# FFN-down with ten of sixteen contraction pairs a sweep by seven products, in threes, with half of their weight sums made earlier and kept in HBM

## The chip, the cores and the metric

One core of one Trainium2 chip runs the whole program. The metric is the device time of one execution in microseconds (us), as the median of several runs.

## What is computed

One decoder layer over 256 tokens of width 2048 in float32. Its parts are a pooling and RWKV-7 mixer, a squared-ReLU MLP with inner width 8192, and a gated embedding behind it. Only the MLP changes, and of it mainly the second product:

```python
h2 = rms_norm(x, mlp_norm[i])
x = x + jnp.square(jax.nn.relu(h2 @ w_ffn_up[i])) @ w_ffn_down[i]
gate = jax.nn.sigmoid(rms_norm(x, ple_norm[i]) @ w_ple_gate[i])
x = x + gate * (p[i] @ w_ple_proj[i])
```

## The kernel before

**Three matmuls for one product.** Every float32 operand is split into a high part (ScalarE copies it to the type that TensorE takes, line 171 for weights) and a low part (VectorE subtracts the high part from the original, line 172). One product of two operands is then three matmuls: high by high, low by high, and high by low.

**The MLP in two halves.** `ffn_half` does FFN-up for half of the inner width (eight calls of `gemm_wide`, tiles `wh_u`, `wl_u`, lines 1121 and 1125), squares the result into 16 activation pairs that it keeps in SBUF, and then runs two sweeps of FFN-down, each for 1024 of the 2048 output columns. The sweeps are named d00, d01, d10 and d11 (half, then column block). In the trace all four share the name `d`.

**A sweep.** Its 16 pairs are 2 x 128 rows of the contraction each. For a pair two raw weight tiles of 128x1024 are loaded, `ra` with the blocks b11 and b22 and `rb` with b12 and b21. A *plain* pair takes eight products of 128x512, 24 matmuls. A pair in `SEVEN` is done in the manner of Strassen and Winograd: seven products, 21 matmuls, on sums of the activation blocks (made in `square_seven`) and on four sums of weight blocks (`weights_seven`). Before the change the odd pairs 1 to 13 are in `SEVEN`, so that a plain pair stands between any two. Within a seven TensorE first takes the three *block products* (p1, p2, p3, weights `w7h`, `w7l`) and then the four *sum products* (weights `th`, `tl`): eight matmuls with `th`, then four with `tl`. The sums are made in a tile `t` (lines 1244, 1247, 1248), its high parts `th` by ScalarE (1249, 1253), its low parts `tl` by VectorE (1254). There is one buffer each of `t`, `th` and `tl`.

**Rings.** Raw weight tiles come from a ring of five buffers, their high parts `wh` from a ring of five, their low parts `wl` from a ring of four. A tile gets the buffer of the one taken five (four) places earlier, so it waits until that one's last reader is done. SyncE's queue (SP) issues all the weight loads in order.

**PSUM.** A sweep adds up in four banks (p2, p3, p4, d22) and in two double banks w1 (p1, p6) and w2 (p5, p7). Behind the last seven the double banks are joined in a tile `u` (lines 1306 to 1308) and added to the residual stream `x` (line 1327, 128x1024). Behind the last pair the four banks are added to `x` (line 1327, 128x512), one by one. The next sweep takes the same four banks in the same order, so its first matmul on p2 waits until VectorE has taken p2 away.

**What sets the order.** From FFN-up on, a scheduler places the instructions on each engine in an order of its own, by priorities and by estimates of when each is ready. The engines then run that list strictly in order. An instruction that waits holds up all that is listed behind it on its engine.

## Time and profile before

| | us |
|---|---|
| median of three runs (lowest, highest) | 1178.73 (1176.62, 1181.19) |
| the profiled execution, its own time | 1176.96 |
| its span, first to last instruction | 1175.2 |
| TensorE busy in the span | 1159.9 |
| VectorE busy | 855.4 |
| ScalarE busy | 673.2 |

The profiled execution has 1.76 us outside its span and lies 1.77 us under the median of the runs. "PE" in the rows below is TensorE, "DVE" VectorE, "ACT" ScalarE, "SP" SyncE. Matmuls overlap: a 128x512 one is shown 389 ns long, but the distance from one to the next is shorter, so durations of matmuls are read from starts.

### The profile page before, as it was taken

What the parts mean: (1) busy time and instruction counts of PE and PEld (TensorE: products, weight loads), DVE (VectorE), ACT (ScalarE), POOL (GpSimd) and SP (SyncE); (2) the same over time, 40 slices, a digit from 0 to 9 for tenths busy, and PEclk for the clock granted to TensorE, in tenths of its full rate; (3) what the DMA queues carried; (4) which work ended last, traced back from release to release, by engine and by line L of the source; (5) the groups of instructions that cost most, each with busy time, mean ns of one, the idle gap of its engine ahead of it and who ended that gap; (6) DMA issues with size and microseconds to landing.
All of it is one profiled execution on the core that took longest, in us unless ns stands there. A gap on an engine that the chain in (4) does not pass through costs nothing.

```text
span 1175.2 us, 18983 instructions
## 1 busy us (share of the span) xinstructions
PE 1159.9 (99%) x7384; PEld 998.0 (85%) x7384; DVE 855.4 (73%) x1073; ACT 673.2 (57%) x1208; POOL 18.3 (2%) x77
## 2 busy tenths in 40 slices
...
GB/s 271 162 171 127 156 144 141 150 169 142 202 182 182 192 184 193 190 188 195 185 191 198 216 214 215 182 190 184 186 190 174 188 221 205 215 253 171 294 98 72
DMA packets 60906, 216.92 MB, mean 185 GB/s; under 512 B 6800, under 2 KB 7696, under 8 KB 60432
## 3 DMA queue, kind: packets, MB, share of 16 engines
...
## 4 chain that ended last, share of the span: by engine, by line
PE 86%; DVE 2%; ACT 1%; DMA 0%; issue 0%; DVEq 0%; ACTq 0%
PE u_w L1121 20%; PE d_p L1191 17%; PE u_w L1125 10%; PE d_w L1191 6%; PE d_d L1191 4%; PE o_b L194 2%; PE o_b L195 2%; PE o_b L193 2%; PE gt_b L193 2%; PE gt_b L195 2%; PE gt_b L194 2%; PE zp_b L193 1%; PE zp_b L195 1%; PE zp_b L194 1%; PE zv_b L184 1%; PE zv_b L186 1%
## 5 line engine op out<-in xcount | busy, mean ns | idle before, releaser
L1121 PE MATMUL u_w<-h,wh_u 128*128 128x512 f32 x1024 | 358.7, 395 | 0.0
L1125 PE MATMUL u_w<-h,wl_u 128*128 128x256 f32 x1024 | 287.3, 281 | 0.0
L171 ACT ACTIVATE wh_u<-raw_u 128x512 fp32r<-128x512 f32 x256 | 147.3, 624 | 157.7 <-issue 134.1
L172 DVE TENSOR_TENSOR wl_u<-raw_u,wh_u 128x1024 fp32r<-128x1024 f32 x128 | 156.4, 1224 | 101.9 <-PE u_w L1125 82.2
L1121 PEld LDWEIGHTS u_w<-h,wh_u 128*128 128x128 f32 x1024 | 192.0, 188 | 44.9
L1125 PEld LDWEIGHTS u_w<-h,wl_u 128*128 128x128 f32 x1024 | 193.5, 189 | 0.0
L171 ACT ACTIVATE wh_d<-raw_d 128x512 fp32r<-128x512 f32 x144 | 82.2, 622 | 64.4 <-PE d_d L1191 45.2
L1191 PE MATMUL d_p<-wh_d,yd 128*128 128x512 f32 x432 | 115.5, 389 | 0.0
L1191 PEld LDWEIGHTS d_p<-wh_d,yd 128*128 128x128 f32 x432 | 81.0, 188 | 16.8
L172 DVE TENSOR_TENSOR wl_d<-raw_d,wh_d 128x1024 fp32r<-128x1024 f32 x72 | 85.3, 1219 | 6.7 <-PE d_d L1191 4.7
L1254 DVE TENSOR_TENSOR tl_d<-t_d,th_d 128x2048 fp32r<-128x2048 f32 x28 | 64.1, 2290 | 16.6 <-ACT th_d L1253 16.6
L1191 PE MATMUL d_p<-wl_d,yd 128*128 128x512 f32 x216 | 66.5, 389 | 0.0
L172 DVE TENSOR_TENSOR wl_o<-raw_o,wh_o 128x1024 fp32r<-128x1024 f32 x32 | 39.1, 1223 | 37.5 <-PE o_b L195 21.8
L171 ACT ACTIVATE wh_o<-raw_o 128x512 fp32r<-128x512 f32 x64 | 36.9, 624 | 38.6 <-issue 17.8
L1191 PEld LDWEIGHTS d_p<-wl_d,yd 128*128 128x128 f32 x216 | 40.5, 188 | 8.5
L1243 ACT ACTIVATE w7h_d<-raw_d 128x1024 fp32r<-128x1024 f32 x28 | 29.5, 1054 | 26.8 <-PE d_d L1191 25.4
L1244 DVE TENSOR_TENSOR t_d<-raw_d,raw_d 128x1024 f32<-128x1024 f32 x28 | 34.2, 1221 | 14.6 <-DMA raw_d<-in_w_ffn_down_dram 14.5
L1191 PE MATMUL d_w<-th_d,ys 128*128 128x512 f32 x168 | 42.6, 389 | 0.0
L1249 ACT ACTIVATE th_d<-t_d 128x1024 fp32r<-128x1024 f32 x28 | 29.7, 1062 | 20.5 <-ACT wh_d L171 8.4
L1253 ACT ACTIVATE th_d<-t_d 128x1024 fp32r<-128x1024 f32 x28 | 29.5, 1053 | 20.6 <-DVE t_d L1248 20.6
L172 DVE TENSOR_TENSOR wl_zp<-raw_zp,wh_zp 128x1024 fp32r<-128x1024 f32 x16 | 19.5, 1221 | 26.0 <-ACT wh_zp L171 24.8
L1191 PE MATMUL d_d<-wh_d,yd 128*128 128x512 f32 x144 | 38.5, 389 | 0.0
...
## 6 DMA issues: line engine op xcount, KB each, us to landing
raw_u<-in_w_ffn_up_dram SPq DMA_DIRECT2D x128, 512.0 KB, 3.5
raw_d<-in_w_ffn_down_dram SPq DMA_DIRECT2D x128, 512.0 KB, 4.3
raw_o<-in_w_out_dram SPq DMA_DIRECT2D x32, 512.0 KB, 3.6
raw_gt<-in_w_ple_gate_dram SPq DMA_DIRECT2D x24, 512.0 KB, 4.6
raw_zk<-in_w_in_dram SPq DMA_DIRECT2D x16, 512.0 KB, 3.5
raw_zr<-in_w_in_dram SPq DMA_DIRECT2D x16, 512.0 KB, 3.5
raw_zv<-in_w_in_dram SPq DMA_DIRECT2D x16, 512.0 KB, 3.5
raw_zp<-in_w_in_dram SPq DMA_DIRECT2D x16, 512.0 KB, 3.5
```

What stands on the lines that cost most here:

```text
L171: nc.scalar.activation(wh[:, a * 512 : (a + 1) * 512], raw[:, a * 512 : (a + 1) * 512], AF.Copy)
L172: nc.vector.tensor_tensor(wl, raw, wh.bitcast(F32), op=ALU.subtract)
L193: nc.tensor.matmul(o, a_h, wh[:, 0:n], start=first, stop=False)
L194: nc.tensor.matmul(o, a_l, wh[:, 0:n], start=False, stop=False)
L195: nc.tensor.matmul(o, a_h, wl[:, 0:n], start=False, stop=last)
L1121: nc.tensor.matmul(bank[:, ct, :].rearrange("p (s t) -> p s t", s=2), wh[:, c], hl, start=k == 0, stop=False, skip_group_check=True,)
L1125: nc.tensor.matmul(bank[:, ct, 0:T], wl[:, c], hl[:, 0, :], start=False, stop=k == 15, skip_group_check=True)
L1191: nc.tensor.matmul(o, l, r, start=first, stop=last, skip_group_check=True)
L1243: nc.scalar.activation(ha, ra, AF.Copy)
L1244: nc.vector.tensor_tensor(t[:, 0:2], ra.rearrange("p (c n) -> p c n", c=2), b12.unsqueeze(1).to_broadcast([128, 2, 512]), op=ALU.subtract)
L1249: nc.scalar.activation(th[:, 0:2], t[:, 0:2], AF.Copy)
L1254: nc.vector.tensor_tensor(tl, t, th.bitcast(F32), op=ALU.subtract)
```

## The change

`SEVEN` becomes all pairs but 0, 3, 6, 9, 12 and 15: ten a sweep, and two of them now follow each other without a plain pair between. Of each two neighbours the second (2, 5, 8, 11, 14, named `AHEAD`) no longer makes its weight sums in the sweep. `sums_ahead` makes them during FFN-up: it loads both raw tiles through the raw ring, makes the four sums on VectorE in a tile that shares the buffer of `th`, and writes them, 1 MB, to a DRAM tile. The sweep reads them back as two raw tiles, and reads only half of `rb`. The first neighbour (1, 4, 7, 10, 13) makes its sums in place, over the raw tiles, after their low parts are taken. The first neighbour does its sum products first and its block products after, the second the other way round. `t` is gone. `u` (and the scratch tile of `rms_stat`) share the buffer of `tl` instead. The activation sums are made in place as well. The weights that `keep` holds for the last gate product are put into other buffers, and their low parts are made in two instructions instead of one.

```diff
-    SEVEN = tuple(range(1, 14, 2))
-    F_A11, F_A12, F_A22, F_S1, F_S3, F_S2, F_S4 = range(7)
+    PLAIN = tuple(range(0, 16, 3))
+    AHEAD = tuple(range(2, 16, 3))
+    SEVEN = tuple(i for i in range(16) if i not in PLAIN)
+    dr = ctx.enter_context(tc.tile_pool(name="dr", bufs=1, space=bass.MemoryType.DRAM))
+    saved = {}
...
+    def sums_ahead(hf, np_, i):
+
+        ra, rb = (
+            load_raw(w_down[np_, hf * 16 + i, r].rearrange("p a n -> p (a n)"), 1024, f"ta{hf}{np_}_{i}_{r}") for r in range(2)
+        )
+        b11, b22, b12, b21 = ra[:, 0:512], ra[:, 512:1024], rb[:, 0:512], rb[:, 512:1024]
+        t = fp.tile([128, 4, 512], F32, tag="th", name=f"ta{hf}{np_}_{i}")
+        with tc.high_priority(20000):
+            nc.vector.tensor_tensor(
+                t[:, 1:3], ra.rearrange("p (c n) -> p c n", c=2)[:, ::-1], b12.unsqueeze(1).to_broadcast([128, 2, 512]),
+                op=ALU.subtract,
+            )
+            nc.vector.tensor_tensor(t[:, 0], b11, t[:, 1], op=ALU.add)
+            nc.vector.tensor_tensor(t[:, 3], b21, t[:, 0], op=ALU.subtract)
+        d_ = saved[hf, np_, i] = dr.tile([128, 2, 1024], F32, tag=f"ta{hf}{np_}_{i}", name=f"tad{hf}{np_}_{i}")
+        nc.sync.dma_start(d_.rearrange("p r n -> p (r n)"), t.rearrange("p c n -> p (c n)"))
+    F_A11, F_A12, F_A22, F_S2, F_S3, F_S4, F_S1 = range(7)
 
...
     def square_seven(src, pr):
 
-        y = fp.tile([128, 1792], F32R, tag="ys", bufs=7, name=f"ys{pr}")
+        if pr == SEVEN[-1]:
+            y = a8(5, f"ys{pr}", F32R)[:, 0:1792]
+        else:
+            y = fp.tile([128, 1792], F32R, tag="ys", bufs=9, name=f"ys{pr}")
         yh, yl = (y[:, c : c + 896].rearrange("p (f t) -> p f t", t=128) for c in (0, 896))
         k1t0, k1t1, k2t0, k2t1 = (src[:, c * 128 : (c + 1) * 128] for c in range(4))
-        sf = fp.tile([128, 4, 128], F32, tag="u", name=f"sf{pr}")
-        nc.vector.tensor_tensor(sf[:, 0], k1t1, k2t1, op=ALU.add)
-        nc.vector.tensor_tensor(sf[:, 1], k1t0, k1t1, op=ALU.subtract)
-        nc.vector.tensor_tensor(sf[:, 2], sf[:, 0], k1t0, op=ALU.subtract)
-        nc.vector.tensor_tensor(sf[:, 3], k2t0, sf[:, 2], op=ALU.subtract)
         tok0 = src.rearrange("p (k t) -> p k t", k=2)[:, :, 0:128]
         split_sb(yh[:, 0:2], yl[:, 0:2], tok0)
         split_sb(yh[:, 2], yl[:, 2], k2t1)
-        split_sb(yh[:, 3:7], yl[:, 3:7], sf)
+        nc.vector.tensor_tensor(k2t1, k1t1, k2t1, op=ALU.add)
+        nc.vector.tensor_tensor(k1t1, k1t0, k1t1, op=ALU.subtract)
+        nc.vector.tensor_tensor(k1t0, k2t1, k1t0, op=ALU.subtract)
+        nc.vector.tensor_tensor(k2t0, k2t0, k1t0, op=ALU.subtract)
+        split_sb(yh[:, 3:7], yl[:, 3:7], src.rearrange("p (f t) -> p f t", t=128))
...
-    def weights_seven(ra, rb, name):
-
-        b12, b21, b22 = rb[:, 0:512], rb[:, 512:1024], ra[:, 512:1024]
-        t, th, tl = (
-            fp.tile([128, 4, 512], dt, tag=tg, name=f"{tg}_{name}") for tg, dt in (("t", F32), ("th", F32R), ("tl", F32R))
-        )
+    def weights_seven(ra, rb, tr, name):
+
+        b11, b22, b12, b21 = ra[:, 0:512], ra[:, 512:1024], rb[:, 0:512], rb[:, 512:1024]
+        th, tl = (fp.tile([128, 2, 1024], F32R, tag=tg, name=f"{tg}_{name}") for tg in ("th", "tl"))
         ha, hb = (ring("wh", F32R, f"w7h{i}_{name}") for i in range(2))
         la, lb = (ring("wl", F32R, f"w7l{i}_{name}") for i in range(2))
         with tc.high_priority(20000):
             nc.scalar.activation(ha, ra, AF.Copy)
-            nc.vector.tensor_tensor(
-                t[:, 0:2], ra.rearrange("p (c n) -> p c n", c=2), b12.unsqueeze(1).to_broadcast([128, 2, 512]), op=ALU.subtract
-            )
-            nc.vector.tensor_tensor(t[:, 2], b22, t[:, 0], op=ALU.add)
-            nc.vector.tensor_tensor(t[:, 3], b21, t[:, 2], op=ALU.subtract)
-            nc.scalar.activation(th[:, 0:2], t[:, 0:2], AF.Copy)
             nc.scalar.activation(hb[:, 0:512], b21, AF.Copy)
             nc.vector.tensor_tensor(la, ra, ha.bitcast(F32), op=ALU.subtract)
             nc.vector.tensor_tensor(lb[:, 0:512], b21, hb[:, 0:512].bitcast(F32), op=ALU.subtract)
-            nc.scalar.activation(th[:, 2:4], t[:, 2:4], AF.Copy)
-            nc.vector.tensor_tensor(tl, t, th.bitcast(F32), op=ALU.subtract)
+            if tr is None:
+                nc.vector.tensor_tensor(b22, b22, b12, op=ALU.subtract)
+                nc.vector.tensor_tensor(b12, b11, b12, op=ALU.subtract)
+                nc.vector.tensor_tensor(b11, b11, b22, op=ALU.add)
+                nc.vector.tensor_tensor(b21, b21, b11, op=ALU.subtract)
+                tr = (ra, rb)
+            for r in range(2):
+                nc.scalar.activation(th[:, r], tr[r], AF.Copy)
+            for r in range(2):
+                nc.vector.tensor_tensor(tl[:, r], tr[r], th[:, r].bitcast(F32), op=ALU.subtract)
 
...
+            kept_sums = saved.get((hf, np_, i))
+            ra = load_raw(src[np_, i, 0].rearrange("p a n -> p (a n)"), 1024, f"{name}_0_{i}")
+            if kept_sums is None:
+                rb, tr = load_raw(src[np_, i, 1].rearrange("p a n -> p (a n)"), 1024, f"{name}_1_{i}"), None
+            else:
+                rb = ring("raw", F32, f"raw_{name}_1_{i}")
+                nc.sync.dma_start(rb[:, 512:1024], src[np_, i, 1, :, 1])
+                tr = [load_raw(kept_sums[:, r], 1024, f"{name}_{2 + r}_{i}") for r in range(2)]
             if i in SEVEN:
-                w = weights_seven(ra, rb, f"{name}_{i}")
+                w = weights_seven(ra, rb, tr, f"{name}_{i}")
                 a = acts[i]
                 fin = i == last_seven
-                for which, o, f, t in (("p1", p1, F_A11, "b11"), ("p2", p2, F_A12, "b21"), ("p3", p3, F_S4, "b22")):
-                    put(which, o, a(f), w[t], fin and which == "p1")
-                for step in (put_high, put_low):
-                    for which, o, f, t in (
-                        ("p5", p5, F_S1, "t1"), ("p7", p7, F_S3, "t3"), ("p6", p6, F_S2, "t2"), ("p4", p4, F_A22, "t4")
-                    ):
-                        step(which, o, a(f), w[t], fin and which != "p4")
+                blocks = [("p1", p1, F_A11, "b11"), ("p2", p2, F_A12, "b21"), ("p3", p3, F_S4, "b22")]
+                sums_ = [("p5", p5, F_S1, "t1"), ("p7", p7, F_S3, "t3"), ("p6", p6, F_S2, "t2"), ("p4", p4, F_A22, "t4")]
+
+                def of_blocks():
+                    for which, o, f, t in blocks:
+                        put(which, o, a(f), w[t], fin and which == "p1")
+
+                def of_sums():
+                    for step in (put_high, put_low):
+                        for which, o, f, t in sums_:
+                            step(which, o, a(f), w[t], fin and which != "p4")
+
+                for part in (of_sums, of_blocks) if i + 1 in SEVEN else (of_blocks, of_sums):
+                    part()
                 if fin:
-                    u = fp.tile([128, 4, 512], F32, tag="t", name=f"u_{name}")
+                    u = fp.tile([128, 4, 512], F32, tag="tl", name=f"u_{name}")
...
             if f == 1:
                 inv_ms()
+            for j in range(i * 5 // 4, (i + 1) * 5 // 4):
+                sums_ahead(hf, j // 5, AHEAD[j % 5])
 
```

VectorE where sweep d00 ends and d01 begins, before. `u_d00` joins the double banks, `x0` and `x1` are the residual stream of the two token blocks, `d00_p2` to `d00_d22` the four banks, `wl_d01_0_0` and `wl_d01_1_0` the low parts for the first pair of d01, and `w7l0_d01_1` that of `ra` for its pair 1. `[waits ...]` names the engines or DMA queues that the row waits for.

```order
L1306 TENSOR_TENSOR u_d00_6540<-d00_w1_5978,u_d00_6540 128x512 [waits Activation_49]
L1307 TENSOR_TENSOR u_d00_6540<-d00_w2_5979,u_d00_6540 128x512 [waits DVE_49]
L1308 TENSOR_TENSOR u_d00_6540<-u_d00_6540,d00_w2_5979 128x2x512 [waits DVE_49]
L1327 SCALAR_TENSOR_TENSOR x0_3441<-u_d00_6540,s2sq_4301,x0_3441 128x1024 [waits DVE_49]
L1327 SCALAR_TENSOR_TENSOR x1_3442<-u_d00_6540,s2sq_4301,x1_3442 128x1024
L172 TENSOR_TENSOR wl_d01_0_0_6638<-raw_d01_0_0_6633,wh_d01_0_0_6637 128x1024 [waits DMAHW1_49,PE_49]
L172 TENSOR_TENSOR wl_d01_1_0_6643<-raw_d01_1_0_6635,wh_d01_1_0_6642 128x1024 [waits DMAHW2_49,PE_49,Activation_49]
L1327 SCALAR_TENSOR_TENSOR x0_3441<-d00_p2_5974,s2sq_4301,x0_3441 128x512 [waits DVE_49,PE_49]
L1327 SCALAR_TENSOR_TENSOR x0_3441<-d00_p3_5975,s2sq_4301,x0_3441 128x512 [waits PE_49]
L1244 TENSOR_TENSOR t_d01_1_6675<-raw_d01_0_1_6671,raw_d01_1_1_6673 128x1024 [waits DMAHW4_49,DMAHW3_49,DVE_49]
L1327 SCALAR_TENSOR_TENSOR x1_3442<-d00_p4_5976,s2sq_4301,x1_3442 128x512 [waits PE_49]
L1327 SCALAR_TENSOR_TENSOR x1_3442<-d00_d22_5977,s2sq_4301,x1_3442 128x512 [waits PE_49]
```

The same place after the change:

```order
L1345 TENSOR_TENSOR u_d00_6720<-d00_w1_6098,u_d00_6720 128x512 [waits Activation_49]
L172 TENSOR_TENSOR wl_d01_0_0_6780<-raw_d01_0_0_6775,wh_d01_0_0_6779 128x1024 [waits DMAHW1_49,Activation_49]
L1346 TENSOR_TENSOR u_d00_6720<-d00_w2_6099,u_d00_6720 128x512 [waits DVE_49]
L172 TENSOR_TENSOR wl_d01_1_0_6785<-raw_d01_1_0_6777,wh_d01_1_0_6784 128x1024 [waits DMAHW2_49,Activation_49]
L1347 TENSOR_TENSOR u_d00_6720<-u_d00_6720,d00_w2_6099 128x2x512 [waits DVE_49]
L1268 TENSOR_TENSOR w7l0_d01_1_6821<-raw_d01_0_1_6813,w7h0_d01_1_6819 128x1024 [waits DMAHW3_49,PE_49,Activation_49]
L1366 SCALAR_TENSOR_TENSOR x0_3441<-u_d00_6720,s2sq_4301,x0_3441 128x1024 [waits DVE_49]
L1366 SCALAR_TENSOR_TENSOR x1_3442<-u_d00_6720,s2sq_4301,x1_3442 128x1024
L1366 SCALAR_TENSOR_TENSOR x0_3441<-d00_p2_6094,s2sq_4301,x0_3441 128x512 [waits DVE_49]
L1366 SCALAR_TENSOR_TENSOR x0_3441<-d00_p3_6095,s2sq_4301,x0_3441 128x512
L1366 SCALAR_TENSOR_TENSOR x1_3442<-d00_p4_6096,s2sq_4301,x1_3442 128x512 [waits DVE_49]
L1366 SCALAR_TENSOR_TENSOR x1_3442<-d00_d22_6097,s2sq_4301,x1_3442 128x512
```

The two low parts for d01's first pair moved in among the three joins, `w7l0_d01_1`, which stood behind all rows on `x`, moved ahead of all six, and it waits for TensorE: its buffer in the ring of four is that of `wl_d00_0_15`, which the last matmul of d00 reads.

VectorE in the middle of sweep d00, before, around pairs 6 and 7 (`t_d00_7` are the sums of pair 7):

```order
L1244 TENSOR_TENSOR t_d00_7_6262<-raw_d00_0_7_6258,raw_d00_1_7_6260 128x1024 [waits DMAHW7_49,DMAHW0_49,DVE_49]
L1247 TENSOR_TENSOR t_d00_7_6262<-raw_d00_0_7_6258,t_d00_7_6262 128x512 [waits DVE_49]
L172 TENSOR_TENSOR wl_d00_0_6_6225<-raw_d00_0_6_6220,wh_d00_0_6_6224 128x1024 [waits DMAHW5_49,PE_49]
L1248 TENSOR_TENSOR t_d00_7_6262<-raw_d00_1_7_6260,t_d00_7_6262 128x512 [waits DVE_49]
L172 TENSOR_TENSOR wl_d00_1_6_6230<-raw_d00_1_6_6222,wh_d00_1_6_6229 128x1024 [waits DMAHW6_49,PE_49,Activation_49]
L1251 TENSOR_TENSOR w7l0_d00_7_6267<-raw_d00_0_7_6258,w7h0_d00_7_6265 128x1024 [waits PE_49]
L1252 TENSOR_TENSOR w7l1_d00_7_6268<-raw_d00_1_7_6260,w7h1_d00_7_6266 128x512 [waits Activation_49]
L1254 TENSOR_TENSOR tl_d00_7_6264<-t_d00_7_6262,th_d00_7_6263 128x2048 [waits PE_49,Activation_49]
L1244 TENSOR_TENSOR t_d00_9_6342<-raw_d00_0_9_6338,raw_d00_1_9_6340 128x1024 [waits DMAHW4_49,DMAHW3_49,DVE_49]
```

After, at pairs 7 and 8 (`raw_d00_0_7` and `raw_d00_1_7` as outputs are the sums in place, `tl_d00_8` are low parts of sums read back):

```order
L1271 TENSOR_TENSOR raw_d00_0_7_6386<-raw_d00_0_7_6386,raw_d00_1_7_6388 128x512 [waits DVE_49]
L1272 TENSOR_TENSOR raw_d00_1_7_6388<-raw_d00_0_7_6386,raw_d00_1_7_6388 128x512 [waits DVE_49]
L1268 TENSOR_TENSOR w7l0_d00_8_6441<-raw_d00_0_8_6429,w7h0_d00_8_6439 128x1024 [waits DMAHW3_49,PE_49,Activation_49]
L1273 TENSOR_TENSOR raw_d00_0_7_6386<-raw_d00_0_7_6386 128x512 [waits DVE_49]
L1269 TENSOR_TENSOR w7l1_d00_8_6442<-raw_d00_1_8_6431,w7h1_d00_8_6440 128x512 [waits DMAHW4_49,PE_49,Activation_49]
L1274 TENSOR_TENSOR raw_d00_1_7_6388<-raw_d00_1_7_6388,raw_d00_0_7_6386 128x512 [waits DVE_49]
L1279 TENSOR_TENSOR tl_d00_7_6391<-raw_d00_0_7_6386,th_d00_7_6390 128x1024 [waits Activation_49]
L1279 TENSOR_TENSOR tl_d00_7_6391<-raw_d00_1_7_6388,th_d00_7_6390 128x1024 [waits Activation_49]
L172 TENSOR_TENSOR wl_d00_1_9_6482<-raw_d00_1_9_6474,wh_d00_1_9_6481 128x1024 [waits DMAHW6_49,PE_49,Activation_49]
L1279 TENSOR_TENSOR tl_d00_8_6438<-raw_d00_2_8_6433,th_d00_8_6437 128x1024 [waits DMAHW5_49,PE_49,Activation_49]
L1268 TENSOR_TENSOR w7l0_d00_10_6518<-raw_d00_0_10_6510,w7h0_d00_10_6516 128x1024 [waits DMAHW7_49,Activation_49]
L1279 TENSOR_TENSOR tl_d00_8_6438<-raw_d00_3_8_6435,th_d00_8_6437 128x1024 [waits DMAHW0_49,Activation_49]
```

The low parts of pair 8 (`w7l0_d00_8`, `w7l1_d00_8`) now stand between the second and the fourth sum of pair 7, and the first of them waits for the buffer of `wl_d00_0_6`, which the plain pair 6 reads to its end. In sweeps d01 and d11 all four sums and `tl` of the first neighbour stand ahead of the second neighbour's rows.

SyncE's queue in FFN-up after the change, around the first saved sums (`raw_ta00_2_0` and `_1` are the loads, `tad00_2` the write). Before, only the `raw_u` rows stand there.

```order
L163 DMA raw_ta00_2_0_4512<-in_w_ffn_down_dram 128x1024 [waits DMAHW4_49,DVE_49]
L163 DMA raw_ta00_2_1_4514<-in_w_ffn_down_dram 128x1024 [waits DMAHW5_49,DVE_49,Activation_49]
L163 DMA raw_u10_0_4523<-in_w_ffn_up_dram 128x1024 [waits DMAHW6_49,DVE_49,Activation_49]
L163 DMA raw_u10_1_4546<-in_w_ffn_up_dram 128x1024 [waits DMAHW1_49,DVE_49]
L163 DMA raw_u10_2_4569<-in_w_ffn_up_dram 128x1024 [waits DMAHW7_49,DVE_49]
L1213 DMA tad00_2_4520<-ta00_2_4516 128x2048 [waits DVE_49]
L163 DMA raw_u10_3_4592<-in_w_ffn_up_dram 128x1024 [waits DMAHW0_49,DVE_49]
L163 DMA raw_u11_0_4631<-in_w_ffn_up_dram 128x1024 [waits DMAHW2_49]
```

The write is listed behind the loads that still find a free buffer of the ring; the load behind it takes the buffer that these sums give back.

44 lines of the change are left out of this document (22 added, 22 removed).

## The prediction

> **What bounds the kernel now.** I read the table of stretches first, then the chain of waits, the groups, the DMA issues, and the order in time at the end of a sweep.
>
> ```profile
> 554.05:636.40 82.35, 82.35 (x365) 68.16 (x364) 69.62 (x67) 45.09 (x66) 0.00 (x0) 1.00 0.58 197
> 636.40:718.60 82.20, 82.20 (x364) 68.05 (x364) 73.37 (x70) 46.09 (x67) 0.00 (x0) 1.00 0.62 208
> 718.60:899.54 180.94, 180.94 (x1026) 157.00 (x1025) 122.39 (x157) 94.00 (x174) 0.00 (x0) 1.00 0.61 188
> 1085.00:1125.00 40.00, 40.00 (x178) 33.15 (x177) 29.98 (x31) 27.84 (x52) 0.00 (x0) 1.00 0.85 286
> 1166.00:1168.00 2.00, 0.89 (x8) 0.68 (x6) 0.47 (x2) 1.00 (x2) 0.00 (x0) 1.00 0.01 2
> 1168.00:1170.00 2.00, 0.00 (x0) 0.00 (x0) 1.66 (x6) 1.76 (x5) 0.00 (x0) 0.73 0.00 0
> ```
>
> Each row has the stretch, its length, busy us of PE, PE's weight loads, DVE, ACT and POOL, the granted clock, the DMA engines' share and GB/s. The first two rows are the sweeps d00 and d01, the third FFN-up of the second half, the fourth a piece of the gate product. TensorE is busy for the whole of every sweep and of FFN-up, so it is the bound there, and a matmul less is time less as long as it stays so. VectorE is next: 70 to 73 of 82 us in a sweep.
>
> ```profile
> 630.93 4.08 PE d_p L1191 x18
> 635.01 1.36 PE d_d L1191 x6
> ...
> L1191 PE MATMUL d_p<-wh_d,yd 128*128 128x512 f32 x432 | 115.5, 389 | 0.0
> ```
>
> In the chain 18 matmuls of a plain pair take 4.08 us: 0.2267 each from start to start, though one is shown 0.389 long. A plain pair is 24 of them, 5.44 us; a seven is 21, 4.76 us (sums 12, 2.72; blocks 9, 2.04).
>
> **What the change saves.** Ten sevens instead of seven, three matmuls less in each of three pairs, four sweeps: 36 x 0.2267 = 8.2 us off, if TensorE never waits.
>
> **VectorE in a sweep.** Durations from the groups:
>
> ```profile
> L172 DVE TENSOR_TENSOR wl_d<-raw_d,wh_d 128x1024 fp32r<-128x1024 f32 x72 | 85.3, 1219 | 6.7 <-PE d_d L1191 4.7 <-ACT wh_d L171 1.9
> L1254 DVE TENSOR_TENSOR tl_d<-t_d,th_d 128x2048 fp32r<-128x2048 f32 x28 | 64.1, 2290 | 16.6 <-ACT th_d L1253 16.6
> L1244 DVE TENSOR_TENSOR t_d<-raw_d,raw_d 128x1024 f32<-128x1024 f32 x28 | 34.2, 1221 | 14.6 <-DMA raw_d<-in_w_ffn_down_dram 14.5
> L1247 DVE TENSOR_TENSOR t_d<-raw_d,t_d 128x512 f32<-128x512 f32 x28 | 19.2, 687 | 0.4
> L1251 DVE TENSOR_TENSOR w7l_d<-raw_d,w7h_d 128x1024 fp32r<-128x1024 f32 x28 | 34.1, 1218 | 0.4 <-PE u_w L1125 0.4
> L1252 DVE TENSOR_TENSOR w7l_d<-raw_d,w7h_d 128x512 fp32r<-128x512 f32 x28 | 19.1, 683 | 0.0
> L171 ACT ACTIVATE wh_d<-raw_d 128x512 fp32r<-128x512 f32 x144 | 82.2, 622 | 64.4 <-PE d_d L1191 45.2 <-issue 9.4 <-DMA raw_d<-in_w_ffn_down_dram 7.9
> L1249 ACT ACTIVATE th_d<-t_d 128x1024 fp32r<-128x1024 f32 x28 | 29.7, 1062 | 20.5 <-ACT wh_d L171 8.4 <-PE d_p L1191 3.6 <-DVE t_d L1244 3.6
> ```
>
> A seven before: 1.22 + 2 x 0.69 + 1.22 + 0.68 + 2.29 = 6.8 us; plain 2 x 1.22 = 2.44. A sweep 7 x 6.8 + 9 x 2.44 = 69.5 us of 82.3. After, a first neighbour has four sums of 128x512 (2.75), the low parts (1.90) and two of 128x1024 (2.44), 7.1 us; a second one only 1.90 + 2.44 = 4.3. A sweep is 5 x 7.1 + 5 x 4.3 + 6 x 2.44 = 71.8 us of 80.2: fuller (90% against 85%), and not the bound by its sum.
>
> **A triple in the steady order (d01, d11).** Take the first neighbour's sums on TensorE at 0, its blocks to 4.76, the second's blocks to 6.8 and sums to 9.52, the plain pair to 14.96. Back to back a 128x1024 costs VectorE 1.13 (2.35 for two, below). The raw buffers close a loop: the first neighbour's last low part frees the buffer of the next plain pair's first load. From there to the next such low part it takes 4.3 (landing, below), 1.2 (two high parts of 0.62), 3.4 (three low parts of 1.13), 0.6 (one of 128x512), 1.9 (three sums), 1.06 (the first `th`) and 2.35 (two low parts): 14.8, against 14.96. So these sweeps stand at balance, with little slack. I take 0.5 us lost in each, 1 us for both (bounds 0, and 0.3 a triple, 3 us for ten).
>
> ```profile
> raw_u<-in_w_ffn_up_dram SPq DMA_DIRECT2D x128, 512.0 KB, 3.5
> raw_d<-in_w_ffn_down_dram SPq DMA_DIRECT2D x128, 512.0 KB, 4.3
> raw_gt<-in_w_ple_gate_dram SPq DMA_DIRECT2D x24, 512.0 KB, 4.6
> ```
>
> **The end of d00 and of d10, the largest term.** VectorE and TensorE there before:
>
> ```profile
> 627.10 0.68 DVE L1306 TENSOR_TENSOR u_d<-d_w,u_d 128x512 f32<-128x512 f32 x1
> 627.82 0.69 DVE L1307 TENSOR_TENSOR u_d<-d_w,u_d 128x512 f32<-128x512 f32 x1
> 628.55 1.22 DVE L1308 TENSOR_TENSOR u_d<-u_d,d_w 128x1024 f32<-128x1024 f32 x1
> 629.80 2.48 DVE L1327 SCALAR_TENSOR_TENSOR x<-u_d,s2sq,x 128x1024 f32<-128x1024 f32 x2
> 632.20 2.35 DVE L172 TENSOR_TENSOR wl_d<-raw_d,wh_d 128x1024 fp32r<-128x1024 f32 x2
> 634.47 1.40 DVE L1327 SCALAR_TENSOR_TENSOR x<-d_p,s2sq,x 128x512 f32<-128x512 f32 x2
> 637.59 0.74 DVE L1327 SCALAR_TENSOR_TENSOR x<-d_d,s2sq,x 128x512 f32<-128x512 f32 x1
> ...
> 636.21 1.07 PE L1191 MATMUL d_p<-wh_d,yd 128*128 128x512 f32 x4
> 641.65 0.61 PE L1191 MATMUL d_w<-w7h_d,ys 128*128 128x512 f32 x2
> ```
>
> d01 begins on TensorE at 636.21. Its first bank, p2, was taken away by 634.47 + 0.74 = 635.2, one microsecond ahead; two plain pairs, 10.9 us, lay behind the last seven, and the joins had that long. Now the last seven is pair 14 and one plain pair, 5.44 us, is left; and in the new list `w7l0_d01_1` stands ahead of all six rows on `x` and waits for the last matmul of d00. Call the end of d00 E. Then: 0.2 (that matmul's end, 0.389 less 0.227 behind its successor's place), 1.13 for `w7l0`, 2.4 for the two wide `x`, 0.74 for p2: p2 is free at E + 4.5, and TensorE, whose next row is d01's first matmul on p2, waits 4.5 us. The other three banks follow 0.66 apart and TensorE needs them 1.36 apart. Behind that it goes on: p3, p4, d22 to E + 6.5, the low part of `rb` to 7.1, four sums to 9.7, the two `th` of 1.06 to 11.0, while the plain pair is over at 4.5 + 5.44 = 9.95. Pair 1 now wants its sums first, where before its blocks gave 2.04 us: one more wait of 1.1 us. Together 5.6 us, at two places: 11.2. Bounds: below, without the wait for TensorE, the joins from E - 5.4 with the two `wl` among them end at E - 0.5, and 2.4 + 0.74 more give 2.7 us a place; above, one low part more ahead of them, 6.8 us. I take the strict reading of the list, 5.6, since VectorE in the rows above runs its rows one behind the other too.
>
> **The other ends.** Behind d11 the first product of the embedding takes p2. VectorE has the joins from about E - 4.7 (`u` now shares the buffer of `tl`, which pair 14's last matmul reads), two `wl` among them, then the wide `x` and p2: 0.7 + 0.7 + 1.2 + 2 x 1.13 + 2.4 + 0.74 = 8.0, so E + 3.3, less 0.7 of transposes that TensorE now does meanwhile: 2.6 us (bounds 0, all of it hidden, and 3.3). Behind d01 FFN-up needs only the double banks: E + 6.5 + 1.1 for `wl_u80_3`, wanted at E + 3 x 2.83 = 8.5 (180.94 us for 64 raw tiles): nothing, with 0.9 us of cover.
>
> **The first sweeps, d00 and d10.** The list lets low parts of the second neighbour stand between the first's sums. At pair 7: `w7l0_d00_8` waits for the plain pair's end (0 here), then 1.13, a sum 0.6, 0.6, a sum 0.7, and the second `th` 1.05: ready at 4.4, while TensorE has done four of the six block products by 2.72 and wants the first `th` then: 1 to 1.5 us lost. At pair 8 TensorE's new list takes what is ready first and I find no wait. I take 1.5 us a sweep, 3 in all (bounds 0 and 1.5 a triple, 15).
>
> **FFN-up.**
>
> ```profile
> L1226 DVE TENSOR_TENSOR sf<-sf,r 128x128 f32<-128x128 f32 x7 | 2.0, 283 | 0.0
> ```
>
> A saved sum costs VectorE 1.22 + 2 x 0.69 = 2.6 us, ten a half, 26; three more activation pairs with four sums of 0.28 and a split of 0.7, 5.5: 122.4 becomes 154 of 180.9, hidden behind TensorE. The ring must bring 84 raw tiles instead of 64, one each 2.15 us, and SyncE's queue has ten writes of 1 MB between; each waits for its sums, and the load behind it needs the buffer of these sums anyway. The piece of the gate product above runs one raw tile each 2.0 us at full TensorE. Bytes: (84 x 0.524 + 10 x 1.05) MB / 180.9 us = 301 GB/s against 188. The same row shows 286 GB/s, all reads, at a share of 0.85. If 286 were all there is, a half would take 190.6 us, 9.7 more, 19 for both. I take 0.5 us, since an earlier stretch (10 to 20 us) shows more:
>
> ```profile
> 10.00:20.00 10.00, 9.51 (x44) 7.59 (x43) 8.26 (x16) 5.80 (x14) 8.59 (x20) 1.00 0.87 347
> ```
>
> In a sweep the load is (16 x 1.05 + 5 x 0.79) MB / 80.2 us = 258 GB/s, below both. The five activation sums in place, `junk` and the other buffers of `keep` cost nothing that I can see: ScalarE and VectorE have idle time in both places (94 and 122 of 181 us busy).
>
> **Sum.** -8.2 + 11.2 + 2.6 + 3 + 1 + 0.5 = +10.1 us. Against the profiled execution's 1176.96 this is 1187.1; the runs' median is 1.8 higher, and I set 1188.
>
> **Rivals.**
> - *TensorE stays fed, faster.* For: no engine's sum exceeds its stretch, and no row of the sweeps before has TensorE waiting. Against: p2's cover before was 1 us and 5.44 us of cover are taken off. It decides itself at p2's release: if that comes before E, the whole 8.2 us are kept: 1169 to 1171.
> - *No change.* Both ends cost their lower bound, 2 x 2.7, the third 1, the rest 1: 7.4 against 8.2, so 1176 to 1179.
> - *Transfers.* FFN-up is starved at 286 GB/s: up to 19 us more, 1195 to 1207. For: the ring is short by two buffers during saved sums. Against: the 347 GB/s row.
> - *The clock.* In the row from 1166 TensorE is busy for 0.89 us and then stops, and in the row from 1168 the granted clock is 0.73. If it falls in each of the three longer waits and stays so for as long as the wait, 4.5 x 0.27 = 1.2 us more at each, partly hidden by the wait for `th`: 1 to 4 us, 1189 to 1192.
>
> By the Trainium skill ("TensorE: Matmul & The Clock Gate", Part 1: The HAM clock gate) the clock is halved after about 3.4 us of idleness and needs as long a busy stretch to come back. By that rule, as an estimate from this page, a wait of 4.5 us may cost up to 1.7 us more, and three of them 5, which would make 1193. The granted-clock rows agree that it falls within 3 us of idleness; no row shows how it comes back.
>
> **Chances.** A measurement of this kernel tells a change from none at about 0.5%, 5.9 us: under 1172.8 is faster, over 1184.6 slower. Forecast 0.42, clock 0.14, transfers 0.08: slower 0.64. No change 0.22. Faster 0.14. The range of eight in ten leaves out most of the faster case and the upper part of the transfers: 1174 to 1199. It takes in the bounds of the ends (2.7 to 6.8 us each) and first sweeps of up to 5 us each.
>
> **What would show it.** TensorE waiting for VectorE's `x<-d_p` twice, 4 to 5 us each, some 80 us behind each FFN-up, and then about 1 us for `th`; a wait of 2 to 3 us behind d11; matmuls in the sweeps at 0.2267 us and 36 fewer; FFN-up still 181 us. I am wrong if `x<-d_p` ends ahead of the sweep's end, if TensorE idles inside the triples by more than 5 us a sweep, or if FFN-up is longer.

## The result, and the profile after

| | us | against the kernel before |
|---|---|---|
| kernel before, median (lowest, highest) | 1178.66 (1176.62, 1181.19) | |
| changed kernel, median (lowest, highest) | 1231.82 (1229.69, 1234.82) | 1.0452, 95% interval 1.042 to 1.0484 |
| span of the profiled execution, before and after | 1175.2 and 1228.7 | +53.5 |

The change makes the kernel 53 us slower. The direction was forecast, the size was not: 10 us were. The head of the page of the changed kernel, with its DMA issues:

```profile
span 1228.7 us, 19262 instructions
...
PE 1177.2 (96%) x7348; PEld 991.6 (81%) x7348; DVE 927.2 (75%) x1225; ACT 699.4 (57%) x1220; POOL 18.3 (1%) x77
...
raw_u<-in_w_ffn_up_dram SPq DMA_DIRECT2D x128, 512.0 KB, 5.6
raw_d<-in_w_ffn_down_dram SPq DMA_DIRECT2D x108, 512.0 KB, 5.4
...
raw_d<-tad SPq DMA_DIRECT2D x40, 512.0 KB, 4.5
```

The 36 matmuls are gone (7348 of 7384). A raw tile of weights in a sweep now takes 5.4 us to land by the median, where the page of before has 4.3; a tile of saved sums (`tad`) takes 4.5.

The table of stretches of the changed kernel, cut where one stage ends and the next begins. The columns are those of the prediction's first fence: stretch, length, busy us of PE, PE's weight loads, DVE, ACT and POOL, granted clock, DMA share, GB/s.

```profile
375.07:556.81 181.74, 181.74 (x1032) 157.70 (x1033) 147.21 (x206) 97.71 (x185) 0.00 (x0) 1.00 0.80 285
556.81:652.52 95.71, 84.43 (x357) 64.98 (x355) 77.94 (x84) 54.17 (x70) 0.00 (x0) 0.99 0.70 244
652.52:740.91 88.39, 85.32 (x355) 67.20 (x355) 72.33 (x77) 50.36 (x66) 0.00 (x0) 0.97 0.66 229
740.91:922.66 181.75, 181.16 (x1026) 156.86 (x1024) 148.14 (x204) 92.53 (x175) 0.00 (x0) 1.00 0.83 288
922.66:1022.48 99.82, 85.38 (x356) 64.74 (x355) 79.95 (x86) 54.83 (x71) 0.00 (x0) 1.00 0.71 236
1022.48:1111.53 89.05, 85.09 (x354) 66.63 (x355) 72.12 (x78) 50.18 (x65) 0.00 (x0) 0.98 0.64 226
1111.53:1228.70 117.17, 105.41 (x513) 88.69 (x511) 72.73 (x106) 68.44 (x134) 0.00 (x0) 0.95 0.49 168
```

The lengths of the same stages, side by side (from such tables of each kernel; "six buffers" is the first experiment below; a sweep runs to the next stage's first matmul, so a wait at its end counts with it):

| stage | before | after | six buffers |
|---|---|---|---|
| FFN-up, first half | 178.42 | 181.74 | 178.38 |
| d00 | 82.32 | 95.71 | 84.34 |
| d01 | 82.28 | 88.39 | 86.58 |
| FFN-up, second half | 180.89 | 181.75 | 181.17 |
| d10 | 82.34 | 99.82 | 83.54 |
| d11 | 82.28 | 89.05 | 83.99 |
| the rest, to the end | 111.20 | 117.17 | 113.63 |

All four sweeps are longer, though each has nine matmuls less: 354 x 0.2267 = 80.25 us is what TensorE needs for one. TensorE is busy in FFN-up but for 0.6 us, with the loads in at 285 to 288 GB/s, so it isn't starved. TensorE's waits, from the list of waits (engine, line, what it waited for, us in all, times, longest):

```profile
PE d_w L1217 <- ACT th_d L1277: 17.7, 23, 2.5
PE d_p L1217 <- DVE x L1366: 9.0, 2, 4.5
PE pp_b L193 <- DVE x L1366: 3.0, 1, 3.0
PE d_p L1217 <- ACT wh_d L171: 1.9, 3, 1.1
PE d_p L1217 <- DVE wl_d L172: 1.9, 4, 1.0
...
```

The second and third row are the ends of the sweeps, as forecast: 4.5 us twice, and 3.0 behind d11. The first row is new in size. The rows count only time in which no matmul is shown, so the sweeps lose more than these rows add up to: the last matmul ahead of a wait is shown 0.39 us long, and behind one for `th` the second starts 0.34 us after the first. What `th` itself waits for is seen in the chain of waits. One triple of d01 in it, in order of time (start, us, what):

```profile
679.12 5.76 DMA raw_d<-in_w_ffn_down_dram
...
684.96 1.08 ACT w7h_d L1266
...
686.06 0.14 DVE w7l_d L1268
686.20 1.00 issue
687.20 0.68 DVE w7l_d L1269
687.89 0.61 DVE raw_d L1271
...
688.52 0.70 DVE raw_d L1272
...
689.25 0.70 DVE raw_d L1273
...
690.06 1.07 ACT th_d L1277
...
691.15 0.92 DVE tl_d L1279
...
692.11 1.43 PE d_w L1217 x5
693.54 0.45 PE d_p L1217 x2
694.00 0.65 PE d_w L1217 x3
694.65 0.61 DVE w7l_d L1269
...
695.28 6.42 DMA raw_d<-in_w_ffn_down_dram
```

It is a loop. A load lands after 5.8 us, high part, low parts, three sums, `th`, the sum products and the second neighbour's low part follow, and that low part frees the buffer for the same load of the next triple: 695.28 - 679.12 = 16.2 us, where TensorE needs 14.96. One triple of d00:

```profile
580.02 1.22 DVE w7l_d L1268
581.24 1.15 DVE tl_d L1279
...
582.40 5.23 DMA raw_d<-tad
...
587.66 1.07 ACT th_d L1277
...
588.77 1.20 PE d_w L1217 x4
589.97 0.46 PE d_p L1217 x2
590.42 0.46 PE d_w L1217 x2
590.88 4.32 PE d_p L1217 x19
595.20 1.15 PE d_d L1217 x5
...
596.43 1.24 DVE w7l_d L1268
```

Here a saved sum is read (5.2 us) into the buffer that the first neighbour's first `tl` frees; that `tl` stands behind the second neighbour's low part, which waits for the plain pair's last matmul. Again one load in every turn, 596.43 - 580.02 = 16.4 us.

### The profile page after: what moved, and what is told of

Same layout as the page of the kernel before. It is cut to its first block, busy times and chain, and to the rows that moved or that the text cites. A ratio compares the mean times of both kernels' runs of the same rounds, so it can differ in the third digit from the quotient of the medians.

```text
span 1228.7 us, 19262 instructions
## 1 busy us (share of the span) xinstructions
PE 1177.2 (96%) x7348; PEld 991.6 (81%) x7348; DVE 927.2 (75%) x1225; ACT 699.4 (57%) x1220; POOL 18.3 (1%) x77
## 4 chain that ended last, share of the span: by engine, by line
PE 61%; DMA 12%; DVE 10%; ACT 4%; issue 2%; ACTq 0%; DVEq 0%; SPq 0%
PE u_w L1121 17%; DMA raw_d<-in_w_ffn_down_dram 9%; PE u_w L1125 9%; PE d_p L1217 5%; PE d_w L1217 3%; DMA raw_d<-tad 2%; PE o_b L194 2%; PE o_b L193 2%; PE o_b L195 2%; PE gt_b L194 2%; PE gt_b L195 2%; PE gt_b L193 2%; ACT th_d L1277 2%; PE zp_b L193 1%; PE zp_b L195 1%
## 5 line engine op out<-in xcount | busy, mean ns | idle before, releaser
L1277 ACT ACTIVATE th_d<-raw_d 128x1024 fp32r<-128x1024 f32 x80 | 82.7, 1055 | 95.8 <-DVE raw_d L1273 35.9
L1279 DVE TENSOR_TENSOR tl_d<-raw_d,th_d 128x1024 fp32r<-128x1024 f32 x80 | 96.3, 1223 | 40.3 <-ACT th_d L1277 40.1
L1217 PE MATMUL d_p<-wh_d,yd 128*128 128x512 f32 x288 | 82.2, 405 | 11.0 <-DVE x L1366 9.0
L1217 PE MATMUL d_w<-th_d,ys 128*128 128x512 f32 x240 | 68.8, 407 | 17.7 <-ACT th_d L1277 17.7
L172 DVE TENSOR_TENSOR wl_d<-raw_d,wh_d 128x1024 fp32r<-128x1024 f32 x48 | 58.5, 1224 | 25.4 <-ACT wh_d L171 23.6
L1217 PEld LDWEIGHTS d_p<-wh_d,yd 128*128 128x128 f32 x288 | 55.2, 195 | 25.2 <-issue 9.8
L1217 PEld LDWEIGHTS d_w<-th_d,ys 128*128 128x128 f32 x240 | 42.0, 188 | 38.4 <-ACT th_d L1277 31.7
L171 ACT ACTIVATE wh_d<-raw_d 128x512 fp32r<-128x512 f32 x96 | 55.0, 624 | 30.6 <-DMA raw_d<-in_w_ffn_down_dram 30.2
L1217 PE MATMUL d_p<-w7h_d,ys 128*128 128x512 f32 x160 | 50.1, 390 | 1.1 <-ACT w7h_d L1267 1.1
L1268 DVE TENSOR_TENSOR w7l_d<-raw_d,w7h_d 128x1024 fp32r<-128x1024 f32 x40 | 48.9, 1222 | 1.9 <-PE d_d L1217 1.1
```

Of the source, the lines that this page charges most:

```text
L171: nc.scalar.activation(wh[:, a * 512 : (a + 1) * 512], raw[:, a * 512 : (a + 1) * 512], AF.Copy)
L172: nc.vector.tensor_tensor(wl, raw, wh.bitcast(F32), op=ALU.subtract)
L1217: nc.tensor.matmul(o, l, r, start=first, stop=last, skip_group_check=True)
L1268: nc.vector.tensor_tensor(la, ra, ha.bitcast(F32), op=ALU.subtract)
L1277: nc.scalar.activation(th[:, r], tr[r], AF.Copy)
L1279: nc.vector.tensor_tensor(tl[:, r], tr[r], th[:, r].bitcast(F32), op=ALU.subtract)
```

## The experiments

The theories. **A, the ring**: eight raw tiles a triple go through five buffers, and the loss in the sweeps is the wait for a buffer and then for the load. **B**: the single buffers `th` and `tl`, shared by neighbours. **C**: VectorE's order. **D**: what was written to HBM comes back slowly. **Q**: SyncE's one queue holds loads up. Ratios are against the kernel before, on the same chip.

**1. A sixth raw buffer**

```diff
-    RING = {"raw": (3, 2), "wh": (3, 2), "wl": (3, 1)}
+    RING = {"raw": (3, 3), "wh": (3, 1), "wl": (3, 1)}
```

> The changed kernel with a sixth raw buffer; the room for it comes from the ring of high parts, which goes from five to four. Ring theory (A): in every triple one load is on the path, because the buffer it needs comes free only when the first neighbour's last low part is made, and it then takes 5 to 6.4 us to land where I had put 4.3. A sixth buffer lets that load be issued one buffer earlier; of the some 35 us that the four sweeps lose inside the triples 20 to 30 come back: 1200 to 1212 us. Theory B (the single buffers th and tl, shared by two neighbours, hold up the second one) and theory C (VectorE's rows stand in an order that makes it wait): a raw buffer changes neither, 1226 to 1236 us. In the new list the first low part of the new sweep also stands behind the six x rows at the two sweep ends; by the term of my prediction that alone is 1.1 us at each.

Measured: 1190.31 us, 1.0107 (1.0078 to 1.0136): 41 us back. Inside the sweeps, by the table of stages and without the waits for `x` and the half clock behind them, it is 27 us, as A expected; the rest is shorter waits for `x` (2.31 and 1.22 us instead of 4.52 twice), less time at half clock, and a faster FFN-up (4 us, last section). The shares of the chain, first of the changed kernel, then of this one, and this one's chain in d00:

```profile
PE 61%; DMA 12%; DVE 10%; ACT 4%; issue 2%; ACTq 0%; DVEq 0%; SPq 0%
```

```profile
PE 70%; DVE 9%; DMA 4%; ACT 3%; issue 2%; DVEq 0%; ACTq 0%
```

```profile
586.63 4.31 PE d_p L1217 x19
...
601.59 4.31 PE d_p L1217 x19
...
616.55 4.31 PE d_p L1217 x19
```

DMA falls from 12% to 4% of the chain, and in d00 the plain pair now comes each 14.96 us, which is TensorE's own time for a triple to the last digit. In d01 loads stay in the chain, and d01 and d11 still lose 4.6 and 3.7 us. The transfer rate is not what had held the sweeps: 256 GB/s over d00 and d01 against 236 in the changed kernel, while a load lands no sooner (5.2 us for weights and 5.4 for saved sums). So the gain is that loads are issued earlier. B falls: `th` and `tl` are single as before. The engines' lists come out in another order too, so C is not told apart by this run alone.

**2. The cut of the high parts alone**

```diff
-    RING = {"raw": (3, 2), "wh": (3, 2), "wl": (3, 1)}
+    RING = {"raw": (3, 2), "wh": (3, 1), "wl": (3, 1)}
```

> The changed kernel with only the ring of high parts cut from five to four, as in the run with six raw buffers but without the sixth. All theories: the low parts have a ring of four already and are released by the same matmuls, so 1229 to 1238 us. If it is slower than that, the gain of the sixth raw buffer is larger than its run shows.

Measured: 1226.23, 1.0391 (1.0358 to 1.0423). A little less than expected, and its lists differ from the changed kernel's too; the sixth buffer's own part is then 36 us.

**3. The saved sums read from the weights**

```diff
-                tr = [load_raw(kept_sums[:, r], 1024, ...) for r in range(2)]
+                tr = [load_raw(src[np_, i, r].rearrange("p a n -> p (a n)"), 1024, ...) for r in range(2)]
```

> The changed kernel, but in the sweeps the two tiles of saved sums are read from the weights instead of from the tensor that FFN-up wrote to HBM: same number of loads, same bytes, same buffers, other addresses (the second neighbours' sums are then the plain blocks). The writes in FFN-up stay. Theories A, B and C: no difference, 1227 to 1236 us. Theory D (what was written to HBM comes back slowly, or the reads run against the writes): the loads get shorter and the time falls by 10 to 30 us, to 1200 to 1220.

Measured: 1215.9, 1.0314 (1.0291 to 1.0337). The order on PE, VectorE and ScalarE is the same row for row, and raw tiles of the sweeps land in 4.8 us by the median, where all 148 of the changed kernel have 5.2. So the loads' addresses are good for 16 of the 53 us; 37 stay. In the profiled executions 12.5 of the 16 lie within the sweeps; 3 are FFN-up's first half (178.8 us for 181.7), which comes before any changed load. A, too, missed here, since it expected no difference.

**4. The second neighbour without its saved sums**

```diff
-                rb = ring("raw", F32, ...)
-                nc.sync.dma_start(rb[:, 512:1024], src[np_, i, 1, :, 1])
-                tr = [load_raw(kept_sums[:, r], 1024, ...) for r in range(2)]
+                rb = load_raw(src[np_, i, 1].rearrange("p a n -> p (a n)"), 1024, ...)
+                tr = (ra, rb)
```

> The changed kernel, but the second neighbour loads its two weight tiles whole, as every other pair, and takes its high and low sums from these (they are then the plain blocks): six raw tiles a triple instead of eight, and 5 x 0.79 MB less to read in a sweep. ScalarE's and VectorE's rows, th and tl, the order of the products and FFN-up stay. Theory A: with six tiles in a triple the loads run ahead by most of a triple; the stalls inside the triples go almost wholly, 30 to 40 us: 1190 to 1202 us, and what is left is the ends of the sweeps, 9.0 + 3.0 us, and the clock behind them. Theory B or C: nothing of what they blame is changed, 1222 to 1234 us.

Measured: 1196.19, 1.0146 (1.0119 to 1.0173), as A expected. Six tiles a triple in five buffers do nearly what eight in six do. The work of the engines, `th` and `tl` are the changed kernel's, so B falls once more. It also reads less, but run 1 had shown that the rate is not the limit. The lists differ here too; but run 3, with lists that are the same row for row, got 16 us from loads that land 0.4 us earlier, which no theory of the order explains.

**5. Two contiguous pieces**

```diff
-        d_ = ... dr.tile([128, 2, 1024], F32, ...)
+        d_ = ... dr.tile([2, 128, 1024], F32, ...)
```

> The changed kernel, but the tensor of saved sums lies in HBM as two pieces of 512 KB, each contiguous (2 x 128 x 1024), instead of one of 1 MB in which a partition's two 4 KB rows stand side by side (128 x 2 x 1024), so that a load of one half no longer skips 4 KB behind every 4 KB. Same loads, bytes, buffers and order. Reading the weights in their place gave 16 us. If the pitch of 8 KB was the reason (theory D1): 1213 to 1220 us. If it is that the weights' tiles had just been read (D2), or that written data come back slowly (D3): 1227 to 1235 us.

Measured: 1222.25, 1.0374 (1.0351 to 1.0397): 10 us less than the changed kernel, between the two forecasts. In the profiled executions 6 us of it lie within the sweeps. The write of the saved sums changes its layout too, and their loads land in 4.3 us by the median, for 4.5.

**6. The saved sums read from other weights**

```diff
+                tr = [load_raw(w_down[np_, (1 - hf) * 16 + i, r].rearrange("p a n -> p (a n)"), 1024, ...) for r in range(2)]
```

> The changed kernel, with the two tiles of saved sums read from the weights of the other half, which nothing near has read (the sums are then blocks of the wrong pair). Against the run that read the weights of the same pair: D2 (a tile that was just read comes faster): no gain over the changed kernel, 1227 to 1235 us. D1 or D3 (pitch, or written data): the same gain, 1213 to 1220 us.

Measured: 1219.32, 1.0352 (1.0338 to 1.0365). Tiles that nothing had read before give most of the gain of run 3, so D2 falls but for 3 or 4 us by the medians; within the sweeps of the profiled executions run 6 gains the 12 us that run 3 does. The contiguous layout gives 10 of these 12 to 16 us by the medians (the intervals of 5 and 6 overlap), but half of them within the profiled sweeps: the pitch, D1, is part of D, and whether "written data", D3, has the other part is open.

**7. Nine squares, six buffers, two plain pairs at the end**

```diff
-    PLAIN = tuple(range(0, 16, 3))
-    AHEAD = tuple(range(2, 16, 3))
+    PLAIN = (0, 3, 6, 9, 12, 14, 15)
+    AHEAD = (2, 5, 8, 11)
+    RING = {"raw": (3, 3), "wh": (3, 1), "wl": (3, 1)}
...
```

(The places of the last seven's activations and the spread of the saved sums over FFN-up follow from the new numbers.)

> Six raw buffers and four of the high parts, and only nine squares by seven products: pairs 0, 3, 6, 9, 12, 14 and 15 are plain, the sums of pairs 2, 5, 8 and 11 are saved, and two plain pairs stand behind the last seven, pair 13, as in the kernel before. Theory of the ends: with 10.9 us of plain pairs behind the joins TensorE waits at no x row and the clock stays up, which takes 3.5 + 2.2 us of waits and some 3 us of clock from the run with six buffers; 12 matmuls more than with ten sevens, 2.7 us back; one neighbour pair less a sweep, 1 to 2 us less in waits for th: 1178 to 1186 us, level with the kernel before (24 matmuls less than it, 5.4 us). Rival: the first low parts of the new sweep still stand ahead of x rows, and the ends cost what they did with ten: 1188 to 1194 us.

Measured: 1180.68, 1.0026 (1.0016 to 1.0035). No wait for an `x` row behind a sweep is left in the list of TensorE's waits, and the mean granted clock is 0.999 where the changed kernel has 0.991. The theory of the ends holds.

**8. The saved sums issued from GpSimd's queue**

```diff
-                tr = [load_raw(kept_sums[:, r], 1024, ...) for r in range(2)]
+                tr = [ring("raw", F32, ...) for r in range(2)]
+                for r in range(2):
+                    nc.gpsimd.dma_start(tr[r], kept_sums[:, r])
```

> The changed kernel with five raw buffers, its loads of saved sums issued from GpSimd's queue instead of SyncE's. Theory Q (a load whose buffer is free stands behind one that still waits, in the one queue): half or more of the loss in the sweeps goes, 1195 to 1212 us. Ring theory: a load is issued when its buffer comes free, whoever issues it, so within 8 us of the changed kernel: 1224 to 1240 us.

Measured, in one run: 1266.96, 35 us slower than the changed kernel, so neither theory had it. ScalarE's row for `th` waits up to 6.4 us for a saved sum in the sweeps of the first half, where it was 2.8. The lists came out in another order, so this run does not test Q by itself; it gives Q no support. The reason is open.

**9 and 10. Six buffers and the contiguous layout, with nine and with ten squares**

Run 7's and run 1's kernels with the diff of run 5.

> The kernel with nine squares, six raw buffers and two plain pairs at a sweep's end, with the saved sums laid out as two contiguous pieces as in the run on the layout. Same order on all compute engines. It lost some 8 us to waits inside the sweeps against its count of matmuls. If part of them are loads that land late, the layout takes 1 to 4 us: 1176 to 1180 us, level with the kernel before or just under it. If six buffers already run ahead of the loads: no change, 1179 to 1183 us.

> Ten squares, six raw buffers, contiguous layout. Ring theory: what six buffers left (about 6 us of waits for th, 5.7 us of waits for x at the sweep ends and the clock behind the longer of them) is mostly not the loads', so the layout brings little: 1185 to 1191 us. If the landing of the saved sums still sets the triple: 1178 to 1184 us.

Measured: 1180.32, 1.0019 (1.001 to 1.0028), and 1190.51, 1.0103 (1.0084 to 1.0121). Both as without the layout, though the saved sums land sooner: in 4.6 us for 5.2 with nine squares, in 4.8 for 5.4 with ten. A load that lands a little later costs nothing once the ring has a buffer in hand: what runs 3, 5 and 6 took away was part of the same loop.

**11. Nine squares with five buffers**

Run 7 without its line on `RING`.

> Nine squares and two plain pairs at the sweep's end, with the five raw buffers and five buffers of high parts of the changed kernel. Parts it into ends and ring: ends theory: the waits of 4.5, 4.5 and 3.0 us for x rows and the half clock behind them, some 7 us, are gone, 19 us; one triple of five is gone with its share of the ring's loss, 6 to 8 us; 12 matmuls more, 2.7 us: 1231.8 - 19 - 7 + 2.7, 1204 to 1214 us. Rival: the ring's loss at the end of the sweeps only moves into the joins, 1215 to 1230 us.

Measured: 1205.71, 1.0227 (1.0211 to 1.0243). As the ends theory had it. TensorE still waits 17.6 us for `th`; with six buffers (run 7) it is 4.5.

**12. Five buffers of low parts**

```diff
-    RING = {"raw": (3, 2), "wh": (3, 2), "wl": (3, 1)}
+    RING = {"raw": (3, 2), "wh": (3, 1), "wl": (3, 2)}
```

> The changed kernel with five buffers of low parts and four of high parts (instead of four and five). In the first sweeps d00 and d10 the low part of a second neighbour waits for the plain pair's last matmul, which frees its buffer, and the first neighbour's low sums, whose end frees the raw buffer of the next load, stand behind it on VectorE. If that wait is the link that makes d00 and d10 lose 11 and 15 us where d01 and d11 lose 4 to 6: it goes, and 10 to 18 us come back of the 1226 us that the run with four high parts took: 1208 to 1216 us. If the raw buffers alone make the loop: 1222 to 1230 us.

Measured: 1227.74, 1.0426 (1.0404 to 1.0449). Against run 2, which has the same four high parts, a fifth buffer for the low parts brings nothing: that wait in d00's chain does not set the time. What takes its place is open. This run and run 2 also bear on C. The changed kernel, run 2 and run 12 have five raw buffers and three different orders of the lists; their four sweeps, less the waits for `x` and 4 x 80.25, lose 43, 47 and 43 us, half clock included. In runs 1 and 4, with two further orders and room in the ring, it is 14 and 14.

**13 and 14. Seven raw buffers; six without the cut of the high parts**

```diff
-    RING = {"raw": (3, 2), "wh": (3, 2), "wl": (3, 1)}
+    RING = {"raw": (3, 4), "wh": (3, 1), "wl": (3, 1)}   # run 13
+    RING = {"raw": (3, 3), "wh": (3, 2), "wl": (3, 1)}   # run 14
...
-            y = fp.tile([128, 1792], F32R, tag="ys", bufs=9, ...)
+        if pr == SEVEN[-1]:
+            y = a8(5, ...)[:, 0:1792]
+        else:
+            y = fp.tile([128, 1792], F32R, tag="ys", bufs=8, ...)
```

The plain pair 15 then has a 4 KB tile of its own, and `keep` uses that and eight of the `ys`; the rest is run 9's kernel.

> Nine squares, contiguous layout, seven raw buffers and four of the high parts; the room comes from the last plain pair's activations, which take 4 KB of their own while the last seven's go where they were. Ring theory as a count of buffers: five gave 1205.7, six 1180.3; if the loop still is partly the loads', a seventh takes 2 to 4 us more, 1176 to 1179 us; if six already run ahead, nothing: 1179 to 1182 us. Order theory (the sixth buffer won because it happened to change the order of the lists): no steady course, 1175 to 1195 us.

> The same with six raw buffers and five of the high parts: nothing is taken from another ring for the sixth buffer. If the four high parts held something up: 1175 to 1179 us. Ring theory: the gain of the sixth buffer does not hang on the ring of high parts, 1178 to 1182 us.

Measured: 1172.31, 0.9948 (0.9936 to 0.996), and 1177.19, 0.9993 (0.9984 to 1.0002). With nine squares, five, six and seven buffers give 1205.7, 1180.3 and 1172.3: a steady course, better at seven than A had it. (With five, the high parts have five buffers and the saved sums the old layout; with six, that layout makes no difference.) If the order had been the cause, no such course was to be expected; that a part of the 41 us of run 1 is the order's isn't excluded, since no run has a buffer more and the same lists. Giving the high parts their fifth buffer back, with the new places for the activations, brings 3 us. The run with seven buffers is faster than both kernels, by 6 us (0.5%) than the one before. Its page, its shares of the chain, and its waits of TensorE from FFN-up on:

```profile
span 1170.8 us, 19263 instructions
...
PE 1155.7 (99%) x7360; PEld 993.5 (85%) x7360; DVE 904.3 (77%) x1193; ACT 685.9 (59%) x1216; POOL 18.2 (2%) x77
...
PE 83%; DVE 4%; ACT 1%; issue 1%; DMA 0%; DVEq 0%; ACTq 0%
```

```profile
PE d_w L1221 <- ACT th_d L1281: 0.2, 1, 0.2
```

DMA is out of the chain, and TensorE waits 0.2 us for `th` in all four sweeps.

**The ring in one number.** A ring's buffer comes back after (time of a period) x (buffers) / (loads in it). That must hold the landing and the time until the last reader is done:

| kernel | period, loads, buffers | a buffer comes back after | ratio |
|---|---|---|---|
| before | two pairs 10.2 us, 4, 5 | 12.8 us | 1 |
| changed | triple 14.96 us, 8, 5 | 9.4 us | 1.0452 |
| run 1 | 14.96, 8, 6 | 11.2 us | 1.0107 |
| run 4 | 14.96, 6, 5 | 12.5 us | 1.0146 |
| run 13 (nine squares) | 14.96, 8, 7 | 13.1 us | 0.9948 |

(Runs 1 and 4 still have the ends in them.) The number is a first check and ranks no close cases: run 4 has more of it than run 1 and loses as much within its sweeps, and run 14, with 11.2 as in run 1, comes to 0.9993 with nine squares. A first neighbour's tile is held longest, since its sums stand in it until `tl`: the load above is issued at 679.12, and its last reader, the first of two rows on VectorE, ends at about 691.15 + 1.2:

```profile
691.15 2.36 DVE L1279 TENSOR_TENSOR tl_d<-raw_d,th_d 128x1024 fp32r<-128x1024 f32 x2 [0.49 <-ACT th_d L1277]
```

That is 13.2 us of one buffer, where the five give 9.4 on the mean.

## Why the prediction was wrong

Loss within a sweep below is its length less the wait for `x`, less 80.25, and in d01 and d11 less the half clock. It is by far the largest term: 39 us in four sweeps, where 4 were forecast.

| term | forecast | measured |
|---|---|---|
| matmuls saved | -8.2 | -8.2 (329.22 in four sweeps before, less 4 x 80.25) |
| waits for p2 behind d00 and d10 | 2 x 4.5 | 2 x 4.52 |
| wait for `th` behind them | 2 x 1.1 | in the loss of d01 and d11 |
| behind d11 | 2.6 | 3.0 |
| half clock after the three waits | 0 (rival: 1 to 4) | 2.3 + 1.6 + 2.7 |
| loss within d00 and d10 | 1.5 and 1.5 | 10.9 and 15.1 |
| loss within d01 and d11 | 0.5 and 0.5 | 5.9 and 7.2 |
| FFN-up | 0.5 | 3.3 + 0.9 |
| the rest (before FFN-up, behind d11) | 0 | -0.2 |
| sum | +10.1 | +53.5 |

**The step that failed: the raw ring's loop, priced at nearly nothing.** In "A triple in the steady order" (1 us for d01 and d11, measured 13.1) I had seen that the ring closes a loop, and summed it to 14.8 against 14.96, at balance. In "The first sweeps" (3 us for d00 and d10, measured 26) I left it out. Three things in that sum were wrong. The landing: 4.3 was the median of before; on the chain the load takes 5.8 to 6.4. The one at 679.12 is the fourth of four that SyncE issues within 2.9 us; that this makes it long was not tested. The loop: I followed the plain pair's load; the chain goes through the first neighbour's, with TensorE's sum products in it (1.43 + 0.45 + 0.65). And balance was priced as nearly nothing: a loop within 0.2 us of the period had no room for 1.5 us of landing, five times a sweep.

**First sweeps: the cause I named was not the cause.** I let the second neighbour's low parts stand between the first's sums, 1.5 us, with every load already there. The chain has that interleaving in it, but what makes the turn 16.4 us is the load of a saved sum behind it. My upper bound, 7.5 a sweep, was passed in both. With a sixth raw buffer (and that run's other lists) the two lose 1.8 and 2.1 us, so the ring has most of it. Why d10 loses 4 us more than d00 is not settled, nor why the first sweeps lose more than the second; the buffer of the low parts is not the reason (run 12).

**The ends: right.** The strict reading of VectorE's list gave 4.5 and the trace has 4.52 twice; 2.6 came out as 3.0. The following 1.1 us for `th` did not show as a wait: at half clock the plain pair lasted until 660.2, and `th` was ready.

**The clock: a rival in the text, a term in the trace.** The changed kernel behind the first of the waits, TensorE's first row and the stretch; below it the stretch behind d11.

```profile
652.52 2.04 PE L1217 MATMUL d_p<-wh_d,yd 128*128 128x512 f32 x4 [4.52 <-DVE x L1366]
```

```profile
652.50:657.00 4.50, 4.48 (x11) 3.53 (x12) 4.43 (x7) 0.00 (x0) 0.00 (x0) 0.50 0.01 2
...
1115.00:1120.00 5.00, 4.44 (x11) 3.50 (x12) 4.66 (x6) 4.24 (x10) 0.00 (x0) 0.50 0.72 235
```

From start to start, 18 matmuls take 6.35 us where they took 4.08: 2.3 us; the same 18 behind d10 take 5.73, 1.6; behind d11, 13 products take 5.68 instead of 2.95, 2.7. I had taken a clock of 0.73 for as long as the wait; it is 0.50, for 3 to 6 us of work. By the Trainium skill ("TensorE: Matmul & The Clock Gate", Part 1: The HAM clock gate) the clock halves and needs some 3.4 us of work to return. The trace agrees with the half; it has 3.3 us of work at 0.50 behind d10, but 4.6 behind d00 and 5.8 behind d11. My estimate from that page of the Trainium skill, 5 us for three waits, was nearer to the 6.6 measured than my own 1 to 4. I gave it a chance of its own instead of a term, though three of the forecast's waits bring it with them here.

**FFN-up and the transfers rival.** The ring brought its 84 raw tiles a half at 285 to 288 GB/s with no wait of TensorE but 0.6 us: the rival falls. Whether the 3.3 us of the first half are the change's is open (last section).

**VectorE** was forecast at 71.8 us a sweep and has 72.3 and 72.1 in d01 and d11, but 77.9 and 80.0 in d00 and d10. It is not the bound: it is busy for 80 to 82% of each stretch, and the latency of the loop sets the time.

**Two slips of the working** changed nothing: 1187.1 and 1.8 make 1188.9, not 1188, and the piece of the gate product has a raw tile each 1.8 us (22 issues in 40 us), not 2.0.
